# VectorE's order in a two-layer decoder trunk: the inverse's X ahead of taps and masked shares, the last output's classical rows ahead of its upper rows

## The chip, the cores and the metric

The kernel runs on one core of a Trainium2 chip. The metric is the device time of one execution in microseconds (us), taken as the median of several runs. A core has five engines with a queue of instructions each: TensorE (PE, matrix products, which accumulate in PSUM), VectorE (DVE), ScalarE (ACT), GpSimd (POOL) and SyncE (SP). SP's and POOL's queues issue the copies from memory. An engine works through its queue in order; where an instruction needs another engine's result, it waits on a semaphore, and what is queued behind it waits too.

## The reference

Two layers, each with a SwiGLU feed-forward block, a mixing block and a second feed-forward block. All three have a norm that is shifted and scaled from `c`, and a gated residual. The sizes are 512 tokens, width 1024, feed-forward width 2816.

```python
h = h + 0.5 * (1.0 + gt1) * swiglu(hn, w_ffn1_in[l], w_ffn1_out[l])
...
proj = hn @ w_mix_in[l]
p_att, p_rwkv, p_conv = jnp.split(proj, [...], axis=-1)
y_att = sliding_window_sink_attention(p_att, ...)   # blocks of 128 queries, a window of 128 keys, a sink in the softmax
y_rwkv = rwkv7_time_mix(p_rwkv, ...)                # a scan: S = S*w - (S kk)(kk a) + v k;  y = S r
y_conv = short_conv_mix(p_conv, conv_w[l])          # b_gate * conv3(c_gate * h), three taps
mixed = jnp.concatenate([y_att, y_rwkv, y_conv], axis=-1) @ w_mix_out[l]
h = h + (1.0 + gt2) * mixed
...
h = h + 0.5 * (1.0 + gt3) * swiglu(hn, w_ffn2_in[l], w_ffn2_out[l])
```

## The kernel before, in words

Activations lie transposed, features on 128 partitions and tokens along the free axis; the residual stream is eight tiles `h` of 128x512. Every large product is made of three: each operand is split into a rounded high part and a low rest (`wH`, `wL`; `actH`, `actL`; L141 makes the high part on ScalarE, L143 the low one on VectorE), and high x high, high x low and low x high are added in PSUM (L129 to L131 for 512 columns, L434 to L436 for 256). Weight tiles come through rings of a few buffers (`wraw`, `wH`, `wL`); the next load into a buffer waits for its last reader.

Two scheduling layers matter. The kernel is written as Python in the order of the data. A planner inside `mix` interleaves four generators (large products, attention, RWKV scan, inversion) by an estimated clock. Below that the framework schedules the instructions onto the engines, and `issue_after` or `add_manual_dep` with `ORDER` keep one instruction behind another on an engine. `ORDER` adds no wait, only a place in the queue.

**Mixing.** The RWKV scan is computed in chunks of 64 tokens, which needs the inverses of 64x64 triangular matrices. Blocks of 16 are eliminated first, then `invert` doubles them in two levels, `lev` 0 and 1. A level makes products into `ps_x`, masks them on VectorE into `X` (L1124), multiplies `X` by the inverse so far into `ps_t`, and subtracts the result from `T` and its transpose `TT` (L1135). There are two head pairs, so `X` and `TT` exist twice, and each is written in three pieces of 128 or 64 partitions. `ps_x`, `ps_t` and `ps_w` (the first products that use the finished `TT`) share two tags of two PSUM buffers each.

Beside it attention runs for block after block of queries, and per block for two head groups `g`: the softmax's sum `den` is completed and inverted (L1356, L1357), the shares `Sc` are scaled (L1358), TensorE turns them (`ps_pt`), VectorE masks them into `pmc` and, from block 1 on, `pmp` (L1345), and the product with the values goes to `ps_av`. The convolution makes `conv_u` (L923), a first tap (L925) and two more (L926, L927), then multiplies by its gate (L929). All of these are VectorE's.

**The last output.** The last feed-forward block's output product is by a Strassen-like scheme: seven products per half `u` of the output on quarter blocks (`ps_d`, `ps_f`, `ps_g`) with sums of weights (`sum`) and four combinations of activations `P1`, `P2`, `T3`, `T4` (tiles `q`, split into `comH`, `comL`). `last_part` makes the fourth, `T4` (L529, L530, four steps in all, then L141 and L143), for the last product of each half. What is left of the width goes by classical products: `rest_rows(0)` and `rest_rows(1)` make eight tiles `ps_mm`, two PSUM buffers in turn, and VectorE adds each to a tile of `h` (`residual`, L343). `rows_to` adds a quarter's result to two tiles of `h` (L558); the first such rows are those of `s1` (L580, L581).

## Time and profile before

| | us |
|---|---|
| median of three runs | 1797.02 |
| lowest and highest run | 1793.84, 1799.68 |
| the profiled execution | 1795.08 |
| its span, first to last instruction | 1793.3 |
| TensorE busy in it | 1764.2 |
| VectorE busy | 1383.6 |
| ScalarE busy | 856.4 |
| mean granted TensorE clock | 0.999 |

A row of the timeline gives the start and the duration in us, the engine, the line of the kernel, the operation, the output and inputs by the program's names (numbers of buffers left out) with the shapes, and how many instructions the row merges; in brackets stands how long the engine sat idle before, and what ended that. On VectorE and TensorE the next row may start before the last one's duration is over, because such instructions overlap at their ends: the distance between starts is what a place in the queue costs. A row of the waits gives the total, the number of times and the longest.

### The profile page before, as it was taken

What the parts mean: (1) busy time and instruction counts of PE and PEld (TensorE: products, weight loads), DVE (VectorE), ACT (ScalarE), POOL (GpSimd) and SP (SyncE); (2) the same over time, 40 slices, a digit from 0 to 9 for tenths busy, and PEclk for the clock granted to TensorE, in tenths of its full rate; (3) what the DMA queues carried; (4) which work ended last, traced back from release to release, by engine and by line L of the source; (5) the groups of instructions that cost most, each with busy time, mean ns of one, the idle gap of its engine ahead of it and who ended that gap; (6) DMA issues with size and microseconds to landing.
All of it is one profiled execution on the core that took longest, in us unless ns stands there. A gap on an engine that the chain in (4) does not pass through costs nothing. (4 is left out here: it accounts for less than half of the span.)

```text
span 1793.3 us, 34028 instructions
## 1 busy us (share of the span) xinstructions
PE 1764.2 (98%) x13952; PEld 1613.4 (90%) x13952; DVE 1383.6 (77%) x2224; ACT 856.4 (48%) x1324; POOL 148.3 (8%) x233
## 2 busy tenths in 40 slices
PE   9999999999999999999999999999999999999998
PEld 7898999987778999899899989999876798999998
DVE  7877678877768877677888777887686788864897
ACT  7452355365444554255355515543644345533563
POOL 0101001000000011100100010010000000010000
PEclk9999999999999999999999999999999999999999
DMA  9667867522133676877737597773320427684764
GB/s 377 222 183 266 225 193 214 184 88 79 51 111 103 178 190 215 266 195 208 238 116 191 170 308 189 205 227 103 119 71 28 142 80 203 183 245 132 202 165 118
DMA packets 95436, 313.08 MB, mean 175 GB/s; under 512 B 10864, under 2 KB 13168, under 8 KB 94256
## 3 DMA queue, kind: packets, MB, share of 16 engines
q1 hardware_dynamic: 65088, 203.68, 33.5%
q0 software_dynamic: 30192, 107.23, 24.2%
q8 instruction: 109, 1.79, 0.4%
q14 instruction: 47, 0.39, 0.1%
HBM read 306.93 MB, written 3.93 MB: 173 GB/s over the span
## 5 line engine op out<-in xcount | busy, mean ns | idle before, releaser
L141 ACT CAST wH<-wraw 128x1024 fp32r<-128x1024 f32 (+2 forms) x276 | 254.2, 928 | 439.9 <-PE ps_mm L130 200.5
L143 DVE TENSOR_TENSOR wL<-wraw,wH 128x1024 fp32r<-128x1024 f32 (+2 forms) x276 | 295.3, 1074 | 111.6 <-ACT wH L141 110.2
L129 PE MATMUL ps_mm<-actH,wH 128*128 128x512 f32 (+1 forms) x700 | 253.9, 363 | 1.5 <-DVE h L343 1.5
L131 PE MATMUL ps_mm<-actH,wL 128*128 128x512 f32 (+1 forms) x700 | 253.4, 362 | 0.1
L130 PE MATMUL ps_mm<-actL,wH 128*128 128x512 f32 (+1 forms) x700 | 253.3, 362 | 0.0
L129 PE MATMUL ps_mm<-hnH,wH 128*128 128x512 f32 (+1 forms) x712 | 248.5, 354 | 3.3 <-ACT hnH L291 3.0
L130 PE MATMUL ps_mm<-hnL,wH 128*128 128x512 f32 (+1 forms) x712 | 246.3, 347 | 0.3
L131 PE MATMUL ps_mm<-hnH,wL 128*128 128x512 f32 (+1 forms) x712 | 245.3, 346 | 0.6 <-DVE wL L143 0.6
L434 PE MATMUL ps_d<-comH,wH 128*128 128x256 f32 x864 | 239.2, 277 | 0.1
L436 PE MATMUL ps_d<-comH,wL 128*128 128x256 f32 x864 | 238.2, 276 | 0.0
L435 PE MATMUL ps_d<-comL,wH 128*128 128x256 f32 x864 | 238.2, 276 | 0.0
L143 DVE TENSOR_TENSOR wL<-sum,wH 128x1024 fp32r<-128x1024 f32 x110 | 134.6, 1225 | 81.3 <-ACT wH L141 81.2
L141 ACT CAST wH<-sum 128x1024 fp32r<-128x1024 f32 x110 | 115.1, 1047 | 122.8 <-PE ps_f L435 39.2
L199 DVE SCALAR_TENSOR_TENSOR wada<-wada,crep 128x1024 f32<-128x1024 f32 x128 | 153.1, 1220 | 26.0 <-DMA wada<-in_wadaT 25.7
L434 PEld LDWEIGHTS ps_d<-comH,wH 128*128 128x128 f32 x864 | 166.2, 192 | 2.0 <-ACT s L460 1.6
L436 PEld LDWEIGHTS ps_d<-comH,wL 128*128 128x128 f32 x864 | 166.3, 192 | 0.0
L435 PEld LDWEIGHTS ps_d<-comL,wH 128*128 128x128 f32 x864 | 166.3, 192 | 0.0
L129 PEld LDWEIGHTS ps_mm<-hnH,wH 128*128 128x128 f32 x712 | 133.9, 190 | 23.6 <-issue 7.6
L129 PEld LDWEIGHTS ps_mm<-actH,wH 128*128 128x128 f32 x700 | 133.1, 190 | 16.8 <-DVE h L343 1.7
L131 PEld LDWEIGHTS ps_mm<-hnH,wL 128*128 128x128 f32 x712 | 135.8, 191 | 13.7 <-DVE wL L143 1.0
L130 PEld LDWEIGHTS ps_mm<-hnL,wH 128*128 128x128 f32 x712 | 135.8, 191 | 13.1 <-DVE hnL L292 1.3
L131 PEld LDWEIGHTS ps_mm<-actH,wL 128*128 128x128 f32 x700 | 133.1, 190 | 15.6 <-DVE wL L143 0.5
(426 smaller groups left out, 4006.0 us busy)
## 6 DMA issues: line engine op xcount, KB each, us to landing
wada<-in_wadaT POOLq DMA_DIRECT2D x126, 512.0 KB, 4.7
wraw<-in_wmi SPq DMA_DIRECT2D x40, 512.0 KB, 3.5
wraw<-in_w2p SPq DMA_DIRECT2D x36, 512.0 KB, 4.2
wraw<-in_w1p SPq DMA_DIRECT2D x32, 512.0 KB, 4.3
wraw<-in_w1o SPq DMA_DIRECT2D x32, 384.0 KB, 4.7
wraw<-in_w2o SPq DMA_DIRECT2D x32, 384.0 KB, 4.1
wraw<-in_w1o SPq DMA_DIRECT2D x32, 320.0 KB, 3.7
sum<-in_w2p SPq DMA_DIRECT2D x18, 512.0 KB, 4.3
```

Of the source, the lines that this page charges most:

```text
L129: mm(acc, wH, xH, start=start, stop=False)
L130: mm(acc, wH, xL, start=False, stop=False)
L131: latest["large"] = mm(acc, wL, xH, start=False, stop=stop)
L141: latest["cast"] = nc.scalar.copy(hi, src)
L143: return nc.vector.tensor_sub(lo, src, hi.bitcast(F32))
L199: stt(w, w, 1.0, crep, ALU.mult, ALU.mult, accum_out=out_)
L434: mm(acc, wH, xH, start=start and i + k == 0, stop=False, skip_group_check=True)
L435: mm(acc, wH, xL, start=False, stop=False, skip_group_check=True)
L436: mm(acc, wL, xH, start=False, stop=k == 3, skip_group_check=True)
```

## The change

VectorE's instructions get another order in two places; no arithmetic is added or removed.

In mixing, at the inverse's second level (`lev` 1), the last piece of `X` is named as a predecessor of the operations collected in `held`: the second and third tap of the first convolution tile (L926, L927) and the masked shares of attention's block 2. And at level 0 the last subtractions into the second `TT` (collected in `turns`) are placed behind the scaled share of block 2, group 0.

In the last output the addition into `s1` and its two rows of `h`, and the fourth combination (`last_part`), are placed behind the last of the classical rows of half 0 (`classical`).

```diff
@@ strassen_out
-                        residual(pt, 4 * u + i, cg, None)
+                        classical = residual(pt, 4 * u + i, cg, None)
+                    return classical
...
-                    tt(flat(s1), vG, flat(s1), ALU.add)
-                    rows_to(4 * u, cg, lo_, s1)
+                    classical = None
                     if not u:
                         rest_rows(0)
-                        rest_rows(1)
+                        classical = rest_rows(1)
+                    with tc.issue_after(classical.ins) if classical else nullcontext():
+                        tt(flat(s1), vG, flat(s1), ALU.add)
+                        rows_to(4 * u, cg, lo_, s1)
...
                     if not u:
-                        last_part()
+                        with tc.issue_after(classical.ins):
+                            last_part()
@@ mix
-        done = set()
+        done, held, turns = set(), [], []
...
-                stt(cv[:, 1:], u[:, : T - 1], cwp[:, 2 + q : 3 + q], cv[:, 1:], ALU.mult, ALU.add)
-                stt(cv[:, 2:], u[:, : T - 2], cwp[:, q : q + 1], cv[:, 2:], ALU.mult, ALU.add)
+                held.append(stt(cv[:, 1:], u[:, : T - 1], cwp[:, 2 + q : 3 + q], cv[:, 1:], ALU.mult, ALU.add))
+                held.append(stt(cv[:, 2:], u[:, : T - 2], cwp[:, q : q + 1], cv[:, 2:], ALU.mult, ALU.add))
...
-                            tt(X[q][r, e], x, rep(f"lev{lev}", NB)[r], ALU.mult)
+                            new = tt(X[q][r, e], x, rep(f"lev{lev}", NB)[r], ALU.mult)
+                    for later in held if lev else ():
+                        tc.add_manual_dep(later.ins, new.ins.name, ORDER, reason="the inverse goes first")
...
-                                tt(to[q][r, e], to[q][r, e], x, ALU.subtract)
+                                new = tt(to[q][r, e], to[q][r, e], x, ALU.subtract)
+                                if lev == 0 and j == 0 and q == qs[1]:
+                                    turns.append(new)
...
                     made[0] = tt(t.rearrange("p (i q) -> p i q", q=P), pt, rep(name, 4), ALU.mult)
+                    if b == 2:
+                        held.append(made[0])
...
-                    tt(Sc, Sc, den.unsqueeze(2).to_broadcast([P, 4, P]), ALU.mult)
+                    share = tt(Sc, Sc, den.unsqueeze(2).to_broadcast([P, 4, P]), ALU.mult)
+                    for later in turns if (b, g) == (2, 0) else ():
+                        tc.add_manual_dep(later.ins, share.ins.name, ORDER, reason="shares go first")
```

How the built program's queues change is shown at three places. First VectorE in mixing, layer 1, behind the subtractions into the second T. Numbers tell buffers apart: `den_4977`, `Sc_4929` belong to head group 0 of block 2, `den_4990`, `Sc_4930` to group 1. Before:

```order
L1135 TENSOR_TENSOR T1_4518<-T1_4518,ps_t_4998 64x256 x2
L1135 TENSOR_TENSOR TT1_4520<-TT1_4520,ps_t_4997 128x256
L1135 TENSOR_TENSOR TT1_4520<-TT1_4520,ps_t_4998 64x256 x2
L1356 TENSOR_TENSOR den_4977<-den_4977,es_4974 128x4
L1356 TENSOR_TENSOR den_4990<-den_4990,es_4987 128x4
L1357 RECIPROCAL den_4977<-den_4977 128x4
L1357 RECIPROCAL den_4990<-den_4990 128x4
L1358 TENSOR_TENSOR Sc_4929<-Sc_4929,den_4977 128x512
L1358 TENSOR_TENSOR Sc_4930<-Sc_4930,den_4990 128x512
```

And now, the same stretch of VectorE's queue:

```order
L1141 TENSOR_TENSOR T1_4518<-T1_4518,ps_t_4998 64x256 x2
L1366 TENSOR_TENSOR den_4977<-den_4977,es_4974 128x4
L1367 RECIPROCAL den_4977<-den_4977 128x4
L1368 TENSOR_TENSOR Sc_4929<-Sc_4929,den_4977 128x512
L1141 TENSOR_TENSOR TT1_4520<-TT1_4520,ps_t_4997 128x256
L1141 TENSOR_TENSOR TT1_4520<-TT1_4520,ps_t_4998 64x256 x2
L1366 TENSOR_TENSOR den_4990<-den_4990,es_4987 128x4
L1367 RECIPROCAL den_4990<-den_4990 128x4
L1368 TENSOR_TENSOR Sc_4930<-Sc_4930,den_4990 128x512
```

The share of group 0 moved ahead of TT's three pieces, and the two groups' small steps no longer alternate.

Next VectorE's rows that follow at once, from the convolution's product on (`conv_u`, then the taps into `conv_y`; `pmc_5126`, `pmp_5128` are group 0's masked shares, `pmc_5189` group 1's; `X1`, `X0` the two head pairs). Before:

```order
L923 TENSOR_TENSOR conv_u_5099<-ps_mm_4955,conv_c_4947 128x512
L925 TENSOR_SCALAR conv_y_5101<-conv_u_5099,par_93 128x512
L143 TENSOR_TENSOR wL_5373<-wraw_5371,wH_5372 128x1024
L926 SCALAR_TENSOR_TENSOR conv_y_5101<-conv_u_5099,par_93,conv_y_5101 128x511
L1345 TENSOR_TENSOR pmc_5126<-ps_pt_5121,con_83 128x512
L927 SCALAR_TENSOR_TENSOR conv_y_5101<-conv_u_5099,par_93,conv_y_5101 128x510
L1345 TENSOR_TENSOR pmp_5128<-ps_pt_5121,con_83 128x512
L1124 TENSOR_TENSOR X1_4715<-ps_x_5132,con_83 128x256
L1124 TENSOR_TENSOR X1_4715<-ps_x_5133,con_83 64x256 x2
L1124 TENSOR_TENSOR X0_4714<-ps_x_5130,con_83 128x256
L1124 TENSOR_TENSOR X0_4714<-ps_x_5131,con_83 64x256 x2
L1345 TENSOR_TENSOR pmc_5189<-ps_pt_5184,con_83 128x512
```

And now, the part from the weights' low half on:

```order
L143 TENSOR_TENSOR wL_5373<-wraw_5371,wH_5372 128x1024
L1128 TENSOR_TENSOR X1_4715<-ps_x_5133,con_83 64x256
L1128 TENSOR_TENSOR X1_4715<-ps_x_5132,con_83 128x256
L1128 TENSOR_TENSOR X1_4715<-ps_x_5133,con_83 64x256
L1128 TENSOR_TENSOR X0_4714<-ps_x_5131,con_83 64x256
L1128 TENSOR_TENSOR X0_4714<-ps_x_5130,con_83 128x256
L1128 TENSOR_TENSOR X0_4714<-ps_x_5131,con_83 64x256
L930 SCALAR_TENSOR_TENSOR conv_y_5101<-conv_u_5099,par_93,conv_y_5101 128x511
L1353 TENSOR_TENSOR pmc_5126<-ps_pt_5121,con_83 128x512
L931 SCALAR_TENSOR_TENSOR conv_y_5101<-conv_u_5099,par_93,conv_y_5101 128x510
L1353 TENSOR_TENSOR pmp_5128<-ps_pt_5121,con_83 128x512
L1353 TENSOR_TENSOR pmc_5189<-ps_pt_5184,con_83 128x512
```

X's six pieces moved up past two taps and two masked shares; `conv_u`, the first tap and the weights' low half still stand ahead of them. Further on, the low half of a narrower weight tile (`wL_5726`) and the convolution's last step moved behind parts of TT's second set. Layer 2 changes in the same way.

The third place is VectorE in the last output, half 0, behind the last activations (`s_19058` is s1; `sum_19092` is a sum of weights from which, by additions of `first` and `third`, two more are made; `h_85`, `h_87`, `h_89`, `h_91` are pairs of tiles of h). Before:

```order
L529 SCALAR_TENSOR_TENSOR q<-q,actH 128x512
L143 TENSOR_TENSOR wL<-sum_19092,wH 128x1024
L530 TENSOR_TENSOR q<-q,actL 128x512
L580 TENSOR_TENSOR s_19058<-ps_g,s_19058 128x512
L586 TENSOR_TENSOR sum_19092<-sum_19092,first 128x1024
L558 SCALAR_TENSOR_TENSOR h_85<-s_19058,cg,h_85 128x256 x2
L343 SCALAR_TENSOR_TENSOR h_85<-ps_mm,cg,h_85 128x512 x2
L143 TENSOR_TENSOR wL<-sum_19092,wH 128x1024
L343 SCALAR_TENSOR_TENSOR h_87<-ps_mm,cg,h_87 128x512
L591 TENSOR_TENSOR sum_19092<-sum_19092,third 128x1024
```

And now:

```order
L143 TENSOR_TENSOR wL<-sum_19092,wH 128x1024
L589 TENSOR_TENSOR sum_19092<-sum_19092,first 128x1024
L343 SCALAR_TENSOR_TENSOR h_85<-ps_mm,cg,h_85 128x512
L143 TENSOR_TENSOR wL<-sum_19092,wH 128x1024
L343 SCALAR_TENSOR_TENSOR h_85<-ps_mm,cg,h_85 128x512
L594 TENSOR_TENSOR sum_19092<-sum_19092,third 128x1024
L343 SCALAR_TENSOR_TENSOR h_87<-ps_mm,cg,h_87 128x512 x2
L143 TENSOR_TENSOR wL<-sum_19273,wH 128x1024
L343 SCALAR_TENSOR_TENSOR h_89<-ps_mm,cg,h_89 128x512 x2
L343 SCALAR_TENSOR_TENSOR h_91<-ps_mm,cg,h_91 128x512 x2
L586 TENSOR_TENSOR s_19058<-ps_g,s_19058 128x512
L529 SCALAR_TENSOR_TENSOR q<-q,actH 128x512
```

The classical rows (L343) moved up, s1, its rows and the combination's steps behind them; the second classical row now stands behind the second `wL`. Here the scheduler reordered other engines too. TensorE had ten products of `ps_f` between the second and the third classical tile, and three between the fifth and the sixth; now the third follows the second at once, one stands ahead of the fourth and four ahead of the fifth, and 19 are left for the end. ScalarE casts the fourth combination (`comH`) four places later. SP's and POOL's queues keep their order.

## Prediction

> **What bounds the kernel now.** I read the page's busy times first, then what TensorE (PE) waits for, then the timeline at the places where the order changes, and last the granted clock there.
>
> ```profile
> PE 1764.2 (98%) x13952; PEld 1613.4 (90%) x13952; DVE 1383.6 (77%) x2224; ACT 856.4 (48%) x1324; POOL 148.3 (8%) x233
> ```
>
> TensorE is busy for 98% of the span of 1793.3 us. No product is added or removed, so the change can win only what TensorE loses: waits, and time at a reduced clock. In the table of waits (total us, times, longest) three rows name writers that the change moves:
>
> ```profile
> PE ps_t L787 <- DVE X L1124: 4.6, 2, 2.3
> PE ps_pt L787 <- DVE Sc L1358: 1.7, 2, 0.9
> PE ps_mm L129 <- DVE h L343: 1.5, 1, 1.5
> ```
>
> The first two occur once in each layer's mixing, the third in the last output: 7.8 us, 0.43% of the span, is all the waiting there is to take.
>
> **Mixing, layer 1.** First VectorE's rows (start, duration, both in us), in the old order, then TensorE's.
>
> ```profile
> 474.53 1.29 DVE L1135 TENSOR_TENSOR TT<-TT,ps_t 128x256 f32<-128x256 f32 x3
> 475.85 0.24 DVE L1356 TENSOR_TENSOR den<-den,es 128x4 f32<-128x4 f32 x2
> 476.04 0.25 DVE L1357 RECIPROCAL den<-den 128x4 f32<-128x4 f32 x2
> 476.25 1.29 DVE L1358 TENSOR_TENSOR Sc<-Sc,den 128x512 f32<-128x512 f32 x2
> 477.46 0.68 DVE L923 TENSOR_TENSOR conv_u<-ps_mm,conv_c 128x512 f32<-128x512 f32 x1
> 478.19 0.49 DVE L925 TENSOR_SCALAR conv_y<-conv_u,par 128x512 f32<-128x512 f32 x1
> 478.59 1.22 DVE L143 TENSOR_TENSOR wL<-wraw,wH 128x1024 fp32r<-128x1024 f32 x1
> 479.72 0.74 DVE L926 SCALAR_TENSOR_TENSOR conv_y<-conv_u,par,conv_y 128x511 f32<-128x511 f32 x1
> 480.38 0.68 DVE L1345 TENSOR_TENSOR pmc<-ps_pt,con 128x512 f32<-128x512 f32 x1
> 480.99 0.74 DVE L927 SCALAR_TENSOR_TENSOR conv_y<-conv_u,par,conv_y 128x510 f32<-128x510 f32 x1
> 481.64 0.68 DVE L1345 TENSOR_TENSOR pmp<-ps_pt,con 128x512 f32<-128x512 f32 x1
> 482.24 2.59 DVE L1124 TENSOR_TENSOR X<-ps_x,con 128x256 f32<-128x256 f32 x6
> 484.86 0.69 DVE L1345 TENSOR_TENSOR pmc<-ps_pt,con 128x512 f32<-128x512 f32 x1
> 485.47 0.68 DVE L1345 TENSOR_TENSOR pmp<-ps_pt,con 128x512 f32<-128x512 f32 x1
> ```
>
> ```profile
> 477.09 0.63 PE L787 MATMUL ps_pt<-con,Sc 128*128 128x128 f32 x4 [0.87 <-DVE Sc L1358]
> 477.65 1.16 PE L787 MATMUL ps_x<-T,B 64*64 64x64 f32 x64
> ...
> 484.98 1.16 PE L787 MATMUL ps_t<-TT,X 64*64 64x64 f32 x64 [2.29 <-DVE X L1124]
> ...
> 486.92 1.08 PE L787 MATMUL ps_av<-pmc,V 128*64 128x512 f32 x4
> ...
> 491.34 1.98 PE L787 MATMUL ps_w<-AX,TT 64*64 64x128 f32 x64
> ```
>
> *Share ahead of TT.* VectorE is free for the first share at 474.53, where TT stood. From den to its reciprocal is 0.19 and from there to Sc 0.21, so Sc starts at 474.93 and one piece ends 0.69 later, 475.62. TensorE, ready at 477.09 - 0.87 = 476.22, no longer waits: 0.87 won. TT follows at 475.53 (0.60 behind Sc) and ends 1.29 later, 476.82. Here is the first wait that the change adds: the ps_x products write a PSUM buffer that TT reads. They would start at 477.65 - 0.87 = 476.78; the wait passes about 0.15 after TT's end (X ends at 484.83, ps_t starts at 484.98), at 476.97, and it holds from their third product on. I take 0.16 lost, so TensorE is 0.71 ahead.
>
> *X ahead of taps and masked shares.* The second den, reciprocal and share now run in series: 476.83, 477.02, 477.23. conv_u follows at 477.83 (0.37 later than before), conv_y's first step 0.73 on at 478.56, wL at 478.96, X 1.13 behind at 480.09, ending at 482.68. ps_t starts at 482.83, 2.15 earlier than before. TensorE arrives at 484.98 - 2.29 - 0.71 = 481.98 and so still waits 0.85: it is VectorE's queue ahead of X, not only the four moved operations, that is late.
>
> *What stands behind X pays.* The taps and masked shares of the first head group now run after X: 482.71, 483.37, 483.98, 484.63, and then the other group's pmc at 485.23 and pmp at 485.84. Their reader is ps_av. TensorE gets there 1.94 behind ps_t's start, at 484.77; the first pmp ends at 485.31, so the product starts at about 485.46, a new wait of 0.69. The second product needs the other pmc (ends at 485.92) and starts at 486.07. ps_av is four products over 1.86 us (its end is in a row below), 0.465 each, so three more end at 486.07 + 3 x 0.465 = 487.47, against 488.78 before: **1.31 us earlier per layer**. Work from there on is unchanged in order, and TT's second set (2.59 like X's six pieces, with one conv_y step of 0.60 between) ends at 489.63; its reader ps_w moves to 491.34 - 1.31 = 490.03, so it does not wait. The wL that slipped behind TT releases a weight buffer later, but a copy from memory into it has products of two more tiles ahead of its use; I cost this at nothing, and if the cover is gone, it costs the lateness of that one transfer.
>
> Bounds: 0 if the new waits eat all, 0.87 + 2.29 = 3.16 if they are not there. Layer 2 has the same rows. Two layers: 2.62.
>
> **The clock in layer 2.** Each row gives a stretch from ps_t's start to the first large product behind ps_av: length, busy times of PE, PEld, DVE, ACT, POOL, then the clock TensorE was granted.
>
> ```profile
> 484.98:488.78 3.80, 3.80 (x75) 2.00 (x75) 3.77 (x7) 0.00 (x0) 0.00 (x0) 1.00 0.13 17
> 1370.86:1376.30 5.44, 5.44 (x75) 2.51 (x75) 5.07 (x10) 0.00 (x0) 0.00 (x0) 0.69 0.25 77
> ```
>
> The same 75 products took 5.44 - 3.80 = 1.64 us longer in layer 2, at a mean clock of 0.69. Both layers had the same wait ahead, so it is a matter of chance, but of a chance that this nearly empty stretch gives. With the wait cut to 0.85 and a second one of 0.69 apart from it I take it that the clock stays full: 1.64 more. Bounds 0 and, where a falling clock meets both layers instead, -1.64.
>
> [...]
>
> **The last output.** The scheduler also moved TensorE's products: the third classical tile (C) now follows the second (B) at once, where ten ps_f products stood; one ps_f then stands between C and D. The rows:
>
> ```profile
> 1743.58 0.70 DVE L529 SCALAR_TENSOR_TENSOR q<-q,actH 128x512 f32<-128x512 f32 x1
> ...
> 1746.52 1.23 DVE L586 TENSOR_TENSOR sum<-sum,first 128x1024 f32<-128x1024 f32 x1
> ...
> 1748.44 1.42 DVE L343 SCALAR_TENSOR_TENSOR h<-ps_mm,cg,h 128x512 f32<-128x512 f32 x2
> ```
>
> ```profile
> 1746.45 0.27 PE L434 MATMUL ps_f<-comH,wH 128*128 128x256 f32 x1
> ...
> 1747.45 0.28 PE L434 MATMUL ps_f<-comH,wH 128*128 128x256 f32 x1
> 1749.26 0.48 PE L129 MATMUL ps_mm<-actH,wH 128*128 128x512 f32 x1 [1.52 <-DVE h L343]
> 1747.86 1.04 ACT L141 CAST wH<-sum 128x1024 fp32r<-128x1024 f32 x1 [3.77 <-DVE sum L586]
> 1758.60 1.23 DVE L143 TENSOR_TENSOR wL<-sum,wH 128x1024 fp32r<-128x1024 f32 x1
> 1761.39 0.28 PE L434 MATMUL ps_f<-actH,wH 128*128 128x256 f32 x1
> ```
>
> TensorE issued nothing between 1747.56 (0.11 behind its last ps_f) and 1749.26: 1.70. In the new order wL starts at 1743.6, sum at 1744.9, and the first classical row at 1746.0, ending 0.76 later. B's issue ends at 1746.45, so C waits until about 1746.9: 0.45. But the second classical row stands behind another wL, whose cast on ScalarE starts 0.11 behind sum's end at 1746.1 and takes 1.04: wL at 1747.3, the row 1.13 on at 1748.4, ended at 1749.2. TensorE has C (six products, 1.29) and one ps_f until 1748.3, and waits 0.95 for D. That is 1.4 against 1.7, 0.3 won. Behind the last classical row now stand s1, three of the fourth combination's four steps and two rows of h, 4 x 0.60 + 0.79 = 3.2 us, ahead of the wL that ended at 1759.83; its reader, the third ps_f product of the run that begins at 1761.39, gave it 1.8 of cover. With the two steps that stood earlier gone it falls some 0.3 short, which partly goes to another small gap. I take **0.1** in all; bounds -0.9 (half of the 3.2 uncovered beyond the 1.8, and less) and 1.5, the whole wait. The loads on SP's queue into sum buffers follow these wLs: one goes out about 1.7 later, the one ahead of it 2.4 earlier; POOL's accumulating loads stand behind both, so I cost them at nothing; if the later one is late, the end is late by as much, up to 1.7.
>
> **Sum.** 2 x 1.31 + 0.1 + 1.64 = 4.36 us. Against the profiled execution: 1795.08 - 4.36 = 1790.7. That execution lies 1.94 under the median of 1797.02, which I leave as it is: **1792.7 us**, 0.24% less.
>
> **Rivals.** *The clock falls as often as before.* It fell in one of two like stretches, and the new order still leaves two waits near each other. Then only 2.72 is won: 1794.3. *Nothing takes the place of the waits,* VectorE being early enough at ps_av and in the last output: 2 x 3.16 + 1.53 + 1.64 = 9.5, so 1787.5; against it stand the slots above, with X only 2.15 earlier. *The backlog behind X eats the gain:* ps_av is released by the last masked share, not the first; if that chain is 1.3 us longer than I have it, each layer wins nothing; with the clock as before 1796.9. *Slower:* the clock. The new order spreads TensorE's waits over more places (ps_t and ps_av in each layer, C and D in the last output). If two more of these stretches than before fall to the reduced clock, 2 x 1.64 = 3.28 exceeds 2.72: 1797.6. From two on it decides; for it speaks only that one stretch fell already, against it that each new wait is under half of the old. That the change does nothing is excluded by the order of the built program.
>
> **How the numbers follow.** Likeliest 0.48 (its own range 1790.5 to 1794.8), clock as before 0.25, no waits left 0.07, backlog 0.13, slower 0.07. The range from 1789 to 1796.7 leaves out the slower case, half of the backlog's and most of the case without waits. A measurement of this kernel tells about 0.3% from no change, 5.4 us, so under 1791.6 counts as faster. The three runs lie 5.8 us apart, and the likeliest lies 1.1 above that bound: about 0.4 of its chance falls below, with the case without waits and a little of the second 0.30. Over 1802.4 only scatter reaches: 0.04. The rest, 0.66, is no change that can be told.
>
> **What would show it.** Right: ps_pt without a wait; ps_t waiting 0.8 to 0.9 on X in both layers; a new wait of ps_av on pmp or pmc of 0.5 to 0.9; two waits of ps_mm on h, 0.3 and 0.8, in place of 1.5; clock 1.00 in layer 2's stretch. Wrong: no new wait at ps_av (the gain is larger), a ps_w or ps_sc that waits behind the slipped wL, a wait of the last ps_f on wL above 0.5, or a clock under 0.8 in one of the stretches.

## The result and the profile after

The changed kernel takes 1794.06 us (median of 19 runs, 1792.58 to 1795.83). The kernel before, run beside it, takes 1797.29 us (19 runs). The ratio is 0.9977, with an interval from 0.9970 to 0.9984: 3.2 us or 0.23% less, with 4.4 forecast. The profiled execution took 1792.58 us, its span 1790.8. Of the executions behind this document two took far longer, 3397.95 us (kernel before) and 8791.21 us (`e7_order`), and no figure below includes them.

The page's busy times after the change (PEld is TensorE's loading of weights):

```profile
PE 1766.0 (99%) x13952; PEld 1613.3 (90%) x13952; DVE 1384.6 (77%) x2224; ACT 856.5 (48%) x1324; POOL 148.3 (8%) x233
```

TensorE's table of waits (total us, times, longest), the rows that the change touches:

```profile
PE ps_t L791 <- DVE X L1128: 2.2, 2, 1.1
...
PE ps_av L791 <- DVE pmp L1353: 1.1, 2, 0.5
PE ps_mm L129 <- DVE h L343: 1.0, 2, 0.7
```

The wait of `ps_pt` (1.7 before) is gone, that of `ps_t` has fallen from 4.6 to 2.2, `ps_av` has a wait that it did not have, and the one wait of the last output (1.5) has become two of 0.21 and 0.74. Together these are 4.3 us where there were 7.8. Yet the time fell by less than the difference, and the timeline shows why. VectorE in layer 1's mixing:

```profile
476.26 0.17 DVE L1366 TENSOR_TENSOR den<-den,es 128x4 f32<-128x4 f32 x1
...
480.75 1.22 DVE L143 TENSOR_TENSOR wL<-wraw,wH 128x1024 fp32r<-128x1024 f32 x1
482.00 2.60 DVE L1128 TENSOR_TENSOR X<-ps_x,con 64x256 f32<-64x256 f32 x6
...
486.56 0.68 DVE L1353 TENSOR_TENSOR pmp<-ps_pt,con 128x512 f32<-128x512 f32 x1
487.16 0.68 DVE L1353 TENSOR_TENSOR pmc<-ps_pt,con 128x512 f32<-128x512 f32 x1
487.76 0.68 DVE L1353 TENSOR_TENSOR pmp<-ps_pt,con 128x512 f32<-128x512 f32 x1
```

And TensorE in the same stretch, from the last large product ahead of `ps_pt` to the first one behind `ps_av`:

```profile
477.56 0.38 PE L131 MATMUL ps_mm<-hnH,wL 128*128 128x512 f32 x1
477.77 0.60 PE L791 MATMUL ps_pt<-con,Sc 128*128 128x128 f32 x4
478.30 1.48 PE L791 MATMUL ps_x<-T,B 64*64 64x64 f32 x64
...
484.75 1.16 PE L791 MATMUL ps_t<-TT,X 64*64 64x64 f32 x64 [1.09 <-DVE X L1128]
...
487.30 1.24 PE L791 MATMUL ps_av<-pmc,V 128*64 128x512 f32 x3 [0.54 <-DVE pmp L1353]
488.21 0.59 PE L791 MATMUL ps_av<-pmp,V 128*64 128x512 f32 x1
488.38 0.59 PE L791 MATMUL ps_av<-pmc,V 128*64 128x512 f32 x1
488.64 1.19 PE L791 MATMUL ps_av<-pmp,V 128*64 128x512 f32 x3
489.76 0.48 PE L129 MATMUL ps_mm<-hnH,wH 128*128 128x512 f32 x1
```

The same places in the kernel before, where the prediction's rows leave them out:

```profile
475.85 0.38 PE L131 MATMUL ps_mm<-hnH,wL 128*128 128x512 f32 x1
...
487.83 1.03 PE L787 MATMUL ps_av<-pmp,V 128*64 128x512 f32 x4
488.78 0.48 PE L129 MATMUL ps_mm<-hnH,wH 128*128 128x512 f32 x1
```

`ps_av` starts 0.06 behind the end of group 0's `pmp` (486.56 + 0.68 = 487.24). Its eight products are two chains of four, one per head group. Before, they started in pairs, two each at 486.92, 487.40, 487.83 and 488.26. Now they start at 487.30, 487.78, 488.21 and 488.64 for group 0, and at 487.90, 488.38, 488.81 and 489.24 for group 1, whose `pmc` ended at 487.84. (The records do not name the group; it is read from the steps of 0.48, 0.43 and 0.43, which both chains share with the pairs of before.) So neither chain stops on its way, and group 1's `pmp`, which ended at 488.44, holds nothing up. But the second chain starts 0.60 behind the first, and the large product comes 1.86 behind the start of the second, as before behind the start of both. `ps_av` takes 2.46 instead of 1.86, and no row of the waits lists the difference. Another 0.32 goes unlisted at `ps_x`, which now takes 1.41 up to the next large product instead of 1.09.

Each place below is counted from the start of the last large product ahead of `ps_pt` (475.85 before, 477.56 after), so that what happened earlier in the run drops out:

| us behind that product | before | forecast | changed |
|---|---|---|---|
| first `ps_pt` | 1.24 | 0.37 | 0.21 |
| `X` starts on VectorE | 6.39 | 4.24 | 4.44 |
| `ps_t` | 9.13 | 6.98 | 7.19 |
| `ps_av` | 11.07 | 9.61 | 9.74 |
| next large product | 12.93 | 11.62 | 12.20 |

The stretch became 0.73 us shorter, not 1.31. It is 12.20 in layer 2 as well, where it was 14.58 before, 1.64 of that by the reduced clock; so layer 2 gained 2.38. The windows (length, busy times of PE, PEld, DVE, ACT, POOL, the granted clock, share and rate of the transfers) show the clock. Changed kernel:

```profile
349.02:352.43 3.41, 2.23 (x17) 1.76 (x16) 3.41 (x8) 1.76 (x5) 0.99 (x2) 1.00 0.37 109
352.43:355.85 3.42, 3.42 (x19) 3.42 (x18) 3.42 (x10) 1.95 (x4) 0.00 (x0) 0.50 0.24 85
484.75:489.76 5.01, 4.47 (x76) 2.30 (x76) 4.97 (x10) 0.00 (x0) 0.00 (x0) 1.00 0.01 3
1369.33:1374.34 5.01, 4.47 (x75) 2.30 (x76) 4.97 (x10) 0.00 (x0) 0.00 (x0) 1.00 0.02 3
```

The mixing keeps its full clock in both layers. But this execution has a stretch of 3.41 us at half clock elsewhere, at 352.4, behind the norm ahead of layer 1's mixing, where the profile of before had none; it cost 1.6. Summed up by the distance between equal products of the two profiles: +0.2 at the start, +1.6 for the clock at 352, -0.73 and -2.38 in the two mixings, -0.4 and -0.3 at two waits of `ps_o` for which the profile names no releaser (they vary between 0.7 and 1.8 over all profiles), -0.2 in the last output, and -0.3 in small pieces: 2.5 earlier at the end, as the spans say.

The last output after the change, TensorE:

```profile
1744.59 0.48 PE L129 MATMUL ps_mm<-actH,wH 128*128 128x512 f32 x1 [0.21 <-DVE h L343]
...
1745.99 0.27 PE L434 MATMUL ps_f<-comH,wH 128*128 128x256 f32 x1
1747.01 0.48 PE L129 MATMUL ps_mm<-actH,wH 128*128 128x512 f32 x1 [0.74 <-DVE h L343]
```

and VectorE:

```profile
1743.80 0.74 DVE L343 SCALAR_TENSOR_TENSOR h<-ps_mm,cg,h 128x512 f32<-128x512 f32 x1
1745.06 1.23 DVE L143 TENSOR_TENSOR wL<-sum,wH 128x1024 fp32r<-128x1024 f32 x1 [0.52 <-ACT wH L141]
1746.20 0.75 DVE L343 SCALAR_TENSOR_TENSOR h<-ps_mm,cg,h 128x512 f32<-128x512 f32 x1
```

The second classical row stands behind a `wL` that itself waits 0.52 for ScalarE's cast, and TensorE waits for that row.

### The profile page after: what moved, and what is told of

It reads as the page before. It is cut to its first block, busy times and chain, and to the rows that moved or that the text cites. A ratio compares the mean times of both kernels' runs of the same rounds, so it can differ in the third digit from the quotient of the medians.

```text
span 1790.8 us, 34026 instructions
## 1 busy us (share of the span) xinstructions
PE 1766.0 (99%) x13952; PEld 1613.3 (90%) x13952; DVE 1384.6 (77%) x2224; ACT 856.5 (48%) x1324; POOL 148.3 (8%) x233
## 4 chain that ended last, share of the span: by engine, by line
PE 85%; DVE 9%; ACT 3%; issue 2%; DMA 2%; SPq 0%; DVEq 0%; ACTq 0%
PE ps_mm L129 14%; PE ps_mm L130 14%; PE ps_mm L131 14%; PE ps_d L434 7%; PE ps_d L436 7%; PE ps_d L435 7%; PE ps_f L436 3%; PE ps_f L435 3%; PE ps_f L434 3%; DVE wL L143 2%; PE ps_mm L1546 2%; PE ps_g L436 2%; PE ps_g L435 2%; PE ps_g L434 2%; ACT wH L141 1%
```

## The experiments

A letter names a theory throughout. A: VectorE works through its queue without a pause from the end of the inverse's first level to the last masked share, so what counts is how much stands there ahead of what TensorE needs next, and a wait that is taken away reappears at the next such place. B: the first wait, that of `ps_pt`, is the one that counts, and the gain comes from the share ahead of `TT`. C, D, F and G are told where they come up, in the expectations or beside them; in the expectations of `e2_last` and `e8_rows`, C, D and E are also the third, fourth and fifth classical tile, as in the prediction. "Stretch" means the distance of the table above. "Lost by the clock" is an estimate, (1 - mean granted clock) x 1791 us, averaged over the runs; a single run's clock is listed to three places only, which is steps of 1.8 us. Unless said otherwise, diffs are against the changed kernel.

### The two places apart

`e1_mixing` keeps only the order in mixing:

```diff
                     prod(pG, hl(a12), B21, True)
+                    tt(flat(s1), vG, flat(s1), ALU.add)
+                    rows_to(4 * u, cg, lo_, s1)
...
-                    with tc.issue_after(classical.ins) if classical else nullcontext():
-                        tt(flat(s1), vG, flat(s1), ALU.add)
-                        rows_to(4 * u, cg, lo_, s1)
...
-                        with tc.issue_after(classical.ins):
-                            last_part()
+                        last_part()
```

> Only the mixing part of the change (X, shares); the last output as before. Theory A (the stretch of each layer's mixing ends 1.3 us behind VectorE's last masked share): each layer's stretch from ps_pt to the first large product behind ps_av is 0.8 us shorter than before, as in the changed kernel; waits of 1.1 at ps_t and 0.5 at ps_av; the last output keeps its wait of 1.5 us on h. Sum 1.6 us of 1797.3, without what the clock does. Rival B (each of the two moves takes off its own wait and they add up): the same 1.6 here, so this run only gives the part that e3 and e4 must add up to. If the clock gain belongs to the mixing, the median falls by some 0.7 us more than 1.6.

Measured: 1793.14 us against 1795.80, ratio 0.9985 [0.9977, 0.9994]. The stretches are 12.19 and 12.20, the changed kernel's own. In its profile the last output is 1.4 longer than before, because ScalarE waited 1.88 for a weight's landing. Such a late load (1.6 to 2.0) is also in the profiles of `e3_x` and `e9_fill`, which order this place as before, and of `e13_norm`, which orders it as changed; shorter ones (0.9 and 0.6) are in `e11_changed` and `e12_all`. So both orders meet it; whether one meets it more often is not shown by so few profiles.

`e2_last` keeps only the order in the last output:

```diff
-                    for later in held if lev else ():
-                        tc.add_manual_dep(later.ins, new.ins.name, ORDER, reason="the inverse goes first")
...
-                    for later in turns if (b, g) == (2, 0) else ():
-                        tc.add_manual_dep(later.ins, share.ins.name, ORDER, reason="shares go first")
```

> Only the last output's part. Waits of C and D on h of 0.2 and 0.7 in place of one of 1.5, a gap of 0.3 at the third ps_f product of the later run (behind wL); from the classical rows to the end 0.2 us less. Mixing as before: 0.87 at ps_pt and 2.3 at ps_t in each layer. The median falls by 0.2 us; a fall by over 1 would say that the clock gain comes from here.

Measured: 1797.17 us, ratio 1.0005 [0.9996, 1.0014]. Its row in the table of waits:

```profile
PE ps_mm L129 <- DVE h L343: 1.2, 2, 0.7
```

From one product ahead of the last output to the end TensorE takes 54.07 us before, 54.28 here, 53.84 in the changed kernel's first profile and 54.17 in a later one. The reordering of the last output is worth nothing that the runs show, 0.2 either way. What gain the runs do show is the mixing's.

### The two parts of the mixing

`e3_x` has X ahead of taps and masked shares, and nothing else of the change; against `e1_mixing`:

```diff
-                    for later in turns if (b, g) == (2, 0) else ():
-                        tc.add_manual_dep(later.ins, share.ins.name, ORDER, reason="shares go first")
```

> X ahead of taps and masked shares, but the share of the first head group not ahead of TT; last output as before. Theory A: the shares are not in series, so VectorE is 0.37 us earlier at X than in the changed kernel; ps_pt keeps its wait of 0.87, ps_t waits 0 to 0.2, ps_av 0.4, and each layer's stretch is 1.2 us shorter than before, more than the 0.8 of both moves together. Rival B: without the share's 0.87 little is left, a stretch shorter by 0 to 0.4.

Measured: 1791.98 us, ratio 0.9982 [0.9973, 0.9992]. The median is 1.16 under that of `e1_mixing`, but the means are 0.09 apart (1792.90 and 1792.99), with 1.3 and 0.8 lost by the clock; the times do not tell the two apart, the profiles do. TensorE in layer 1:

```profile
477.99 0.38 PE L131 MATMUL ps_mm<-hnH,wL 128*128 128x512 f32 x1
479.25 0.63 PE L788 MATMUL ps_pt<-con,Sc 128*128 128x128 f32 x4 [0.88 <-DVE Sc L1365]
...
484.77 1.16 PE L788 MATMUL ps_t<-TT,X 64*64 64x64 f32 x64
...
487.30 1.24 PE L788 MATMUL ps_av<-pmc,V 128*64 128x512 f32 x3 [0.52 <-DVE pmp L1350]
...
489.75 0.48 PE L129 MATMUL ps_mm<-hnH,wH 128*128 128x512 f32 x1
```

The wait of `ps_pt` stays and that of `ps_t` is gone; the stretch is 11.76, 1.17 shorter than before and 0.44 shorter than in the changed kernel, which has the share part on top.

`e4_shares` has only the share ahead of `TT`; against `e1_mixing`:

```diff
-                    for later in held if lev else ():
-                        tc.add_manual_dep(later.ins, new.ins.name, ORDER, reason="the inverse goes first")
```

> The first share ahead of TT alone; X behind taps and masked shares as before, last output as before. Theory A: the wait of 0.87 at ps_pt goes, but X ends 0.37 us later since the shares run in series, so ps_t waits 2.29 + 0.7 + 0.37 = 3.4 and each layer's stretch is 0.4 us longer than before. Rival B: 0.7 to 0.9 shorter. If the clock falls more often behind a longer wait, the median is more than 0.8 us above before's.

Measured: 1798.87 us, ratio 1.0015 [1.0006, 1.0024], slower than before.

```profile
485.40 1.31 PE L788 MATMUL ps_t<-TT,X 64*64 64x64 f32 x64 [3.48 <-DVE X L1125]
```

`ps_pt` no longer waits, but `ps_t` waits 3.48 in place of 2.29. At full clock it starts 9.58 behind the reference product, 0.45 later than before; then the clock halves in both layers. The windows of `e4_shares`, layer 1:

```profile
482.86:486.27 3.41, 0.87 (x57) 0.90 (x61) 3.31 (x8) 0.00 (x0) 0.00 (x0) 1.00 0.00 0
486.27:489.69 3.42, 3.42 (x28) 1.62 (x20) 3.37 (x8) 0.00 (x0) 0.00 (x0) 0.50 0.22 40
```

The four kernels add up: X ahead is worth -1.17 without the share part (12.93 to 11.76) and, from `e4_shares`'s 9.58 + 1.94 + 1.86 = 13.38 at full clock to 12.20, -1.18 with it. The share part costs 0.45 without X ahead and 0.44 with it. So half of the change in mixing works against the other half. The cause stands in VectorE's queue. With the two groups' small steps in turn (`e3_x`), X starts 5.31 behind `TT`; with one group's share ahead of `TT` and the other's behind it, X starts 482.00 - 476.26 = 5.74 behind `den`, where `TT` would have stood. VectorE in `e3_x`, layer 1:

```profile
476.68 1.29 DVE L1138 TENSOR_TENSOR TT<-TT,ps_t 128x256 f32<-128x256 f32 x3
...
481.99 2.61 DVE L1125 TENSOR_TENSOR X<-ps_x,con 64x256 f32<-64x256 f32 x6
```

X starts where the changed kernel's does, at 482.00, but `e3_x` came to this stretch 0.43 later: TensorE's last large product is at 477.99 against 477.56, and VectorE came free at 476.68 against 476.26. A holds, B falls: what TensorE wins at `ps_pt` it pays at `ps_t`, with 0.45 on top.

### What stands behind X

`e5_taps` puts the two taps behind all four masked shares:

```diff
-                held.append(stt(cv[:, 1:], u[:, : T - 1], cwp[:, 2 + q : 3 + q], cv[:, 1:], ALU.mult, ALU.add))
-                held.append(stt(cv[:, 2:], u[:, : T - 2], cwp[:, q : q + 1], cv[:, 2:], ALU.mult, ALU.add))
+                taps.append(stt(cv[:, 1:], u[:, : T - 1], cwp[:, 2 + q : 3 + q], cv[:, 1:], ALU.mult, ALU.add))
+                taps.append(stt(cv[:, 2:], u[:, : T - 2], cwp[:, q : q + 1], cv[:, 2:], ALU.mult, ALU.add))
...
                         held.append(made[0])
+                        for later in taps:
+                            tc.add_manual_dep(later.ins, made[0].ins.name, ORDER, reason="masked shares go first")
```

> The changed kernel, with the two taps behind all four masked shares instead of between them; nothing else moved by hand. Theory A (VectorE's queue in order of need): ps_av's wait of 0.5 and the waits inside it go, the large product behind ps_av comes 1.2 us earlier than in the changed kernel; but a weight's wL (0.96) now also stands ahead of the inverse's last TT, and TT ends 1 us later, so ps_w waits 1.0 to 1.5 in its place and each layer gains -0.3 to +0.2: the same time as the changed kernel within 0.5 us. Rival C (the waits at ps_av are the whole loss): 1.2 us less per layer, 2.4 us in all.

Measured: 1793.04 us against 1796.69, ratio 0.9981 [0.9970, 0.9992], where the changed kernel has 0.9977. `ps_av` no longer waits and the stretch is 11.00, 1.20 shorter. But TensorE then meets the inverse's second level:

```profile
492.54 1.98 PE L791 MATMUL ps_w<-AX,TT 64*64 64x128 f32 x64 [1.28 <-DVE TT L1141]
```

`ps_w` comes 3.90 behind the large product, with 2.55 in the changed kernel: 1.35 given back for 1.20 won. Behind the masked shares now stood the two taps and a second `wL` ahead of `TT`. The wait moved one place on, as A has it; C, by which the waits at `ps_av` are the whole loss, falls.

`e7_order` writes VectorE's queue in the order in which TensorE needs it: X at once behind the second share, then `conv_u`, the masked shares, `wL`, `TT`, the next `wL`, and only then the convolution.

```diff
         latest["w"] = split(wH[:, :n], wL[:, :n], w[:, :n], behind)
+        if "masked" in latest:
+            latest["masked"].append(latest["w"])
+            if len(latest["masked"]) == 3:
+                tc.add_manual_dep(latest["w"].ins, latest.pop("masked")[0].ins.name, ORDER, reason="masked shares go first")
...
-                tt(pt.like(u), pt.view, pt.like(cc), ALU.mult)
+                held.append(tt(pt.like(u), pt.view, pt.like(cc), ALU.mult))
-                ts(cv, u, cwp[:, 4 + q : 5 + q], None, ALU.mult)
...
+                taps.append(ts(cv, u, cwp[:, 4 + q : 5 + q], None, ALU.mult))
...
                         free[0] = nc.vector.copy_predicated(Sc[:, i0 : i0 + 2], rep("mq", 2).bitcast(I32), pt[:, :, 1])
+                    for later in taps if (b, i0) == (3, 0) else ():
+                        tc.add_manual_dep(later.ins, free[0].ins.name, ORDER, reason="the next block's scores go first")
...
                         held.append(made[0])
+                        latest["masked"] = [made[0]]
```

> The changed kernel with VectorE's queue in the order in which TensorE needs it: second share, X, conv_u, the four masked shares, then the weight's wL that stood ahead of X, TT's last step, the next block's first masks, and only then conv_y's steps. Theory A: X starts when ps_x is done (2.0 us earlier), no wait at ps_t, 0 to 0.3 at ps_av, none at ps_w; the large product behind ps_av 2.3 us earlier than in the changed kernel in each layer, 4.6 us in all, 3.1 us per layer against before. The late wL costs nothing. Rival C: 1.09 + 0.54 per layer, 3.3 us in all. If wL's lateness shows, as a wait on a weight in the next two tiles.

Measured: 1789.10 us (7 runs) against 1796.69, ratio 0.9958 [0.9945, 0.9972]. VectorE and TensorE in layer 1:

```profile
479.31 2.60 DVE L1132 TENSOR_TENSOR X<-ps_x,con 64x256 f32<-64x256 f32 x6
...
484.35 0.68 DVE L1359 TENSOR_TENSOR pmp<-ps_pt,con 128x512 f32<-128x512 f32 x1
...
486.08 2.58 DVE L1145 TENSOR_TENSOR TT<-TT,ps_t 128x256 f32<-128x256 f32 x6
```

```profile
483.16 1.16 PE L795 MATMUL ps_t<-TT,X 64*64 64x64 f32 x64
...
485.10 1.08 PE L795 MATMUL ps_av<-pmc,V 128*64 128x512 f32 x4
...
486.96 0.48 PE L129 MATMUL ps_mm<-hnH,wH 128*128 128x512 f32 x1
```

No wait is left at `ps_pt`, `ps_t`, `ps_av` or `ps_w`. The stretch is 9.83 in both layers: 2.37 shorter than in the changed kernel, 3.10 shorter than before, of the 3.16 that the prediction gave as the bound without new waits. The times agree: by the means the kernel is 7.56 faster than before, of which the clock is 1.52 (2.81 lost against 4.33), which leaves 6.04, near the 2 x 3.10 of the two stretches.

### The last output's rows

`e8_rows` adds to the changed kernel that the second classical row goes ahead of the `wL` and the third ahead of the next sum (`classical` is made a list of the eight rows here):

```diff
-                    prod(pD, hl(S), made["P2"], False)
+                    wS = hl(S)
+                    if not u:
+                        tc.add_manual_dep(latest["parted"].ins, classical[1].ins.name, ORDER, reason="rows go first")
+                    prod(pD, wS, made["P2"], False)
                     nc.scalar.copy(flat(s2), vD)
-                    tt(S, S, a12, ALU.add)
+                    third = tt(S, S, a12, ALU.add)
+                    if not u:
+                        tc.add_manual_dep(third.ins, classical[2].ins.name, ORDER, reason="rows go first")
```

The rival, D, is that what the two tiles win is given back further on.

> The changed kernel with two more moves in the last output: the second classical row ahead of the wL it stood behind, the third ahead of the sum it stood behind. Theory A: D no longer waits (0.74 and some 0.2 of refilling), the wait of C (0.2) and the gap at the third ps_f product (0.3) stay: 0.9 us less than the changed kernel, all of it kept to the end. Rival D: VectorE has as much to do as before, and the time comes back as a wait on wL or on a row behind E: 0 to 0.3 us less.

Measured: 1792.64 us against 1796.69, ratio 0.9974 [0.9963, 0.9984].

```profile
PE ps_mm L129 <- DVE h L343: 0.4, 1, 0.4
```

The wait of the fourth tile is gone, the third waits 0.41. The last output takes 53.15, which is 0.69 less than the changed kernel's 53.84 and 0.92 less than before; nothing is given back. The median alone would not tell this from the changed kernel; the profile does.

`e10_both` is `e7_order` and `e8_rows` together.

> e7_order and e8_rows together: 4.6 + 0.9 = 5.5 us less than the changed kernel by theory A, 3.3 + 0.2 = 3.5 by the rivals. With no wait over 1 us left in the mixing, what is lost by the clock should be no more than in the changed kernel.

Measured: 1787.80 us against 1796.69, ratio 0.9949 [0.9933, 0.9965] from 6 runs, 0.5% under the kernel before: the fastest order found, and under the changed kernel's 0.9977 [0.9970, 0.9984] as well. The stretches are 9.83, the last output 53.32. The clock cost 2.1 per run, where the kernel before, beside it, lost 4.3 and the changed kernel 2.2 and 0.8 in its two sets.

### The clock

`e9_fill` is the kernel before with 14 products of 128x256 ahead of the second `ps_pt`, inside the time that TensorE would wait for X. Their result is overwritten at once, so they only keep TensorE busy. F is the author's theory that the half clock follows a stretch in which TensorE does little, as behind the wait of 2.30 in layer 2 of the kernel before; if so, the dip goes and nothing is lost. Against the kernel before:

```diff
-            def turned(b, Sc):
+            def turned(b, Sc, g):
                 pt = psum([P, 4, P], "ps_pt")
+                for _ in range(14 if (b, g) == (2, 1) else 0):
+                    pe(pt[:, :2], ones_r, ones_r.unsqueeze(1).to_broadcast([P, 2, P]), start=True, stop=True)
...
-                    pm.append(turned(b, Sc))
+                    pm.append(turned(b, Sc, g))
```

> The kernel before, with 14 products of ones by ones (128x256, 0.11 us each, overwritten by the transposes behind them) ahead of the second ps_pt of the third block in each layer: TensorE does 1.55 us of work that serves nothing, in the place of a part of its wait for X. [...] The median is 1 to 2 us below before's, for work added. Rival G (the wait's place or the small 64-row products bring the clock down): the same stretches at half clock, the median within 0.5 us of before's.

Measured: 1799.97 us against 1797.57, ratio 1.0016 [1.0006, 1.0027]. At the place itself the profile fits F:

```profile
481.80 1.83 PE L787 MATMUL ps_pt<-ones_r 128*128 128x256 f32 x14
...
485.99 1.16 PE L787 MATMUL ps_t<-TT,X 64*64 64x64 f32 x64 [0.63 <-DVE X L1124]
```

The wait of 2.29 is down to 0.63, both stretches have full clock and are 12.95 and 12.94, against 12.93: the 1.83 us of products cost nothing there. The median says otherwise. The profile has waits elsewhere that before had not, longest at the sums of squares:

```profile
PE ps_ss L273 <- DVE ss L250: 3.9, 5, 1.2
```

(2.4 in total and 0.6 at most before), with half clock behind three of them, and 0.79 for a late load in the last output. The clock cost 4.8 us per run against 3.5 before, and the rest of the loss is not accounted for. Why these sums came later was not followed. Two stretches at full clock in one profile do not show F, since one of the two kept its clock in the kernel before as well; and that filling the wait helps the kernel is not borne out.

`e11_changed` is the changed kernel again, beside these.

> The changed kernel as it is, beside the others of this call. Theory F: no stretch at half clock in the mixing of either layer; those that there are stand behind the norms (near 350, 573, 907 and 1237 us). 0.2 to 0.3% less than before; what the clock takes is less than before's by 1 to 2 us.

Measured: 1792.74 us against 1797.57, ratio 0.9980 [0.9970, 0.9989]. The means differ by 4.3 (1793.06 and 1797.36); the clock lost 0.81 here and 3.46 before, which is 2.65 of it, and the other 1.65 is the order's. Its profile has no half clock between the first full clock and the end.

`e13_norm` and `e12_all` add four products, whose result is read by nothing, to the sums of squares, the one to the changed kernel and the other to `e10_both`:

```diff
-            pt = psum([P, 2], "ps_ss")
+            pt = psum([P, 2 + 2 * P], "ps_ss")
+            for _ in range(4 if sl.start == 0 and len(sqs) == 1 else 0):
+                m = mm(pt[:, 2:].rearrange("p (a b) -> p a b", b=P), ones_r, ones_r.unsqueeze(1).to_broadcast([P, 2, P]), start=True, stop=True)
+                tc.add_manual_dep(m.ins, latest["large"].ins.name, ORDER, reason="fills the wait")
```

> The changed kernel, with four products of ones by ones (0.44 us) in the wait of 0.6 ahead of the sum of squares, at the three norms near 350, 907 and 1237 us. Theory F: TensorE is busy 2.7 us in the stretch where it was 2.24, no half clock at these three places in any run; the one near 573 us stays possible. What the clock takes falls from some 2 to under 1 us, and the median by 1 to 1.5 us against the changed kernel of this call. Rival G: the waits stay as long as the chain that they wait for, so nothing changes.

Measured: 1795.67 us, ratio 0.9988 [0.9979, 0.9997], 2.9 over `e11_changed`.

```profile
344.25 0.65 PE L270 MATMUL ps_ss<-ones_r 128*128 128x256 f32 x4
```

The products landed at the first half's sum at 344, where TensorE does not wait, and not at the second half's near 350, where it does. There they cost their own 0.5, three times in the kernel, and a half-clock stretch at 353 stayed. By the means the run is 2.4 over `e11_changed`: 1.0 by the clock and 1.4 besides, near the products' 3 x 0.5. The run says nothing on F; it says that products put where TensorE does not wait cost their time.

> VectorE's queue in the order of need in the mixing, the two more rows in the last output, and the four products at the three norms: e10 and e13 together. Theory F and A: 5.5 us less than the changed kernel by the orders and 1 to 1.5 by the clock, some 1787 us where before takes 1797 and the changed kernel 1794; by rival G as e10, 1788.5.

Measured: 1787.82 us, ratio 0.9953 [0.9936, 0.9970], the same as `e10_both`. Its profile has no half clock, but the products' 1.5 us are in it too; with 5 and 6 runs nothing can be told apart here.

## Why the prediction was right, and where it was not

The likeliest case came about: new waits in place of the old ones, a small gain, no clock dip in the mixing. 1792.7 forecast and 1794.06 measured, 4.4 less and 3.2 less; a change of 0.23% is inside the 0.3% that was called no change.

- *Share ahead of TT.* Its steps came as forecast: `ps_pt` without a wait, `ps_x` held back by `TT`. 0.32 was lost there, with 0.16 forecast, and 1.03 won, not 0.87: the restart after the wait had cost TensorE 0.16 more than the wait's row says. What the prediction did not draw from its own line "0.37 later than before" is that this part alone is a loss. `e3_x` and `e4_shares` price it at +0.45 per layer.
- *X ahead.* `ps_t` waits 1.09, with 0.85 forecast. X started 0.20 later than forecast; 0.12 of it is that X follows the `wL` after 1.25, not 1.13. That VectorE's queue ahead of X is what is late was right: `e7_order` took `conv_u`, the first tap and `wL` out of it and the wait was gone.
- *What stands behind X pays.* This is the step that failed, the term of 1.31 per layer, which measured 0.73. The new wait of `ps_av` was right (0.54, with 0.69 forecast). But "so three more end at 486.07 + 3 x 0.465" took `ps_av` for four products one after another, with three left once group 1's `pmc` is there. It is two chains side by side, and the whole of group 1's chain, 1.86, lies behind that `pmc`, not 3 x 0.465 = 1.40: 0.47 more. The late X adds 0.21; the chain starts 0.06 behind the end of `pmc`, not 0.15, which gives 0.09 back. Together this is the 0.58 that was missing, to rounding.
- *The slipped wL* was rightly costed at nothing: `ps_w` follows 2.55 behind the large product, with 2.56 before.
- *The clock.* 1.64 was forecast for layer 2 and came there. That a dip could turn up at another place was not in the sum, and in the profile shown it did, so that the pair of profiles shows nothing won by the clock. Over the runs it holds better: the kernel before lost 3.0, 4.3 and 3.5 us per run by the clock in three sets (88 runs), the changed one 2.2 and 0.8 (30 runs). The weighted means are 3.5 and 1.7, a gain of 1.8; these sets are from several chips, and the one that has both kernels gives 2.65 (`e11_changed`). That 1.64 lies near the mean is luck: it is the price of one dip in one profile of the kernel before, where one of two like places fell.
- *The last output.* 0.1 shorter was forecast; it was 0.23 shorter and 0.10 longer in two profiles of the changed kernel, 0.21 longer in `e2_last`. The waits were 0.21 to 0.42 and 0.74, with 0.45 and 0.95 in the working; the third `ps_f` product lost 0.31 as forecast ("some 0.3 short").
- *Sum.* By the profiles' rows the order is worth 2 x 0.73 + 0.1 = 1.6, with 2.72 forecast, and the clock 1.8 on average, with 1.64 forecast: 3.4 in all, near the 3.2 that the medians show. `e11_changed` has 1.65 and 2.65.

Of the rivals, "nothing takes the place of the waits" needed an order that the change does not have; `e7_order` has it and comes to 3.10 of the 3.16. "The backlog behind X" is near in amount, as 0.58 of the 1.31 was eaten, but not in mechanism: `ps_av` was released by the first `pmp`, and only 0.21 of the 0.58 is VectorE's lateness. "Slower by the clock" came only with the share part alone: `e4_shares`, with one long wait, fell to half clock in both layers and lost 5.4 by it.

Half clock came behind waits of 2.30 (the kernel before in layer 2, `e2_last` in layer 1; not behind 2.29 and 2.30 in the other layer of either) and, at the norms, behind two waits of 0.59 and 0.55 within one stretch (the first window of the changed kernel above: busy for 2.23 of 3.41).

## What to carry to other kernels

When a wait is removed on the engine that bounds the kernel, follow the queue of the engine that it waited for up to the next two or three places where its results are read: as long as that queue has no pause, its whole length up to there is what counts, and a step moved ahead is paid by the readers behind it (0.45 us per layer in `e4_shares`). Order such a queue by when the bounding engine needs each result, splits of weights and side work included; that was worth 7.6 us here (`e7_order`), where the change's moves were worth 3.2. Count what follows a wait by the starts of the single products: two chains that run side by side cost their whole length behind the later one (1.86 us here, with 1.40 forecast). Price each half of a change alone: here one half lost 0.45 us per layer and was carried by the other.

## What the hardware showed that was not expected

*The half clock came in stretches of 3.41 us.* The 14 profiles have 22 of them between the first full clock and the end. The clock records give 3.412 for the one of the kernel before and 3.413 for that of the changed kernel, and in the other profiles windows of 3.41 or 3.42 stand at 0.50. One such stretch cost 1.64 in layer 2 of the kernel before and 1.6 in the changed kernel. The changed kernel's, at 352.43, begins 344.746 us behind the first record of full clock at 7.69, which is 101 times 3.4133; that of the kernel before begins 1365.331 us behind its first, at 6.78, which is 400 times 3.4133. In the seven profiles with two or three stretches they begin 40 to 259 such lengths apart. The windows of the kernel before, the 3.41 us ahead of the place and the next, for both layers:

```profile
481.24:484.65 3.41, 1.44 (x8) 0.94 (x6) 3.34 (x8) 0.83 (x1) 0.00 (x0) 1.00 0.26 101
484.65:488.07 3.42, 3.09 (x73) 2.03 (x75) 3.38 (x7) 0.00 (x0) 0.00 (x0) 1.00 0.02 5
1368.69:1372.11 3.42, 1.25 (x65) 1.22 (x66) 3.34 (x8) 0.52 (x1) 0.00 (x0) 1.00 0.01 2
1372.11:1375.52 3.41, 3.41 (x9) 1.32 (x11) 3.36 (x7) 0.00 (x0) 0.00 (x0) 0.50 0.32 91
```

The same wait lies otherwise in these windows in the two layers: in one TensorE is busy for 1.44 and the next has the clock at 1.00, in the other for 1.25 and the next has 0.50. At three norms (near 350, 907 and 1237 us), with the same products in all 14 profiles and windows laid whole multiples of 3.4133 us behind the first full clock, 13 of the 15 in which TensorE is busy for at most 2.24 us are followed by half clock, and none of the 27 with 2.25 or more. The window of `e10_both` that answers to the changed kernel's at 349.02, with full clock in the next one:

```profile
348.00:351.41 3.41, 2.27 (x19) 2.00 (x18) 3.41 (x8) 1.16 (x3) 0.98 (x2) 1.00 0.10 23
```

So 2.23 us busy went with 1.6 us lost behind it and 2.27 with none; `e11_changed` had 2.23 at this place as well and kept its clock. Where these windows lie differs from run to run: the first full clock came 6.5 to 9.0 us into the span. The clock goes with much of what scatters the runs of one kernel: in the three sets of the kernel before, a run's time and what it lost by the clock have a correlation of 0.85, 0.86 and 0.72. In the mixing the numbers are others: windows with a wait of `ps_t` of 2.3 or more were followed by half clock in four of six (busy 0.87 to 1.35; not at 1.44 and 1.92), windows with 1.1 or less in none of 22. Near 573 us, windows busy for 2.70, 2.75 and 2.79 were followed by half clock (`e8_rows`, `e7_order`, `e5_taps`). So the busy time of the records does not tell these cases apart by itself, and what sets the clock was not shown.

*A wait costs more than its row.* A row counts the idle time from the end of the product ahead, but without the wait the next product would have started before that end. A large product's row lasts 0.38 and the next starts 0.22 behind it; the difference, 0.16, came on top of the wait at two places: 1.03 for 0.87 at `ps_pt`, 0.37 for 0.21 at the third classical tile. By an estimate from these rows two short waits are dearer by 0.16 than one of their sum.
